# Two-layer decoder trunk on one Trainium2 core: four small matmul groups of the first mixer in another order on TensorE

## The chip, the cores and the metric

The kernel runs on one core of a Trainium2 chip, as one launch. The core has five engines that each work through a queue of their own: TensorE (PE, matmuls), VectorE (DVE), ScalarE (ACT), GpSimd (POOL) and SyncE (SP), which here only issues transfers (DMA). They wait for each other through semaphores. The metric is the device time of one execution in microseconds (us); less is better.

## The reference

The input is one sequence of 1024 tokens with 1024 features. Layer 0 has a mixer of two kinds of heads, eight retention heads and eight RWKV-7 heads of 64 features; layer 1 has sliding-window attention. Each layer ends in a SwiGLU network, and all of it is in float32. The change touches only the RWKV-7 heads of layer 0:

```python
def rwkv7_scan(r, w, k, v, a, b):
    def step(state, inp):
        r_t, w_t, k_t, v_t, a_t, b_t = inp
        sa = jnp.einsum('bhij,bhj->bhi', state, a_t)
        state = state * w_t[:, :, None, :] + sa[..., None] * b_t[:, :, None, :] + v_t[..., None] * k_t[:, :, None, :]
        return state, jnp.einsum('bhij,bhj->bhi', state, r_t)
    ...
# in the mixer, behind the shared input projection z = h @ w_in:
y = rwkv7_scan(r_h, heads(decay), k_h, v_h, -kk, kk * heads(a))
y = head_group_norm(y, RWKV_GN_EPS, ln_g, ln_b)
...
return jnp.concatenate([ret_out, rwkv_out], axis=-1) @ w_out
```

The state update of one token needs that of the token before. The kernel doesn't step through tokens: it takes chunks of 64 tokens, turns the updates inside a chunk into small products and one triangular solve, and carries the state from chunk to chunk.

## The kernel before

The 1024 tokens are worked on in two halves of 512 (`hf` 0 and 1). The eight RWKV heads of a half are four pairs `p`; two heads of 64 features fill the 128 partitions (rows), one head in rows 0 to 63, the other in rows 64 to 127 (`half`). Two pairs of one half make a unit `u`: units 0 and 1 are half 0, units 2 and 3 are half 1. A half has `NCH` = 8 chunks.

`pair` (one call for each of the eight pairs) makes, in this order on TensorE: the two small projections of decay and gate (tiles 0 and 1), a sum over each head's features (2), the chunk products of BK and AR called N here (3), which a masking on DVE and transfers through memory (`dn`) bring to the solve, the product of r with `blk` (4), the score groups, two for each half of the chunks, one for each head `e` (tiles 5, 6 and 7, 8; DVE masks them into GG at L887), the transposes of BK for either head (9, 10; ACT copies them into GG at L894), AR's transposition by a product with the identity (11; ACT copies it into `XA[:, :, 0:64]` at L901), the transposes of v (12, 13; DVE makes UV of them at L910 to L930), and GG by UV (14; ACT copies it into the other half of XA at L941).

`unit` solves the triangular systems of its two pairs by 62 steps on DVE, L968 and L972 in turn, on a tile X. Each step needs the one before it. The solved X goes to memory by two stores (`dg<-X`, L976) and comes back in another shape by eight loads (`GT<-dg`, L985); the unit's products with XA, UV and GG follow, and the state goes from chunk to chunk. Retention (lines about L1100 to L1240) runs in streams of its own: L1178 and L1193 are DVE's work between its matmuls, L1215 updates its state Sc, and L1240 stores a result (`cat<-r`). L581 makes normalized input `n` of the second half on DVE for the shared input projection, whose matmuls (`ps_f<-n,w`) fill TensorE between all this. Its split weights are kept in memory (`wsp`) and come back for the second half by L412 (`w<-wsp`).

What sets the order of the work:

- On TensorE, one list written out by hand, `PE_ORDER`. A letter is a stream: F the projection, a the first norm, b to e the units 0 to 3, f and g the pairs of unit 0, h and i those of unit 1, j and k of unit 2, l and m of unit 3, n to q and r to u retention in the first and the second half, v the second norm, W the output projection. `f3:16` takes sixteen matmuls from the fourth tile of stream f; `f5,6:8` takes eight, from the tiles 5 and 6 in turn. `pe_order` chains them in that order.
- A class `Plan` runs the streams as Python generators. It sets in which order instructions and tiles come into being in the program; it keeps an estimate of the time (`now`) and of the PSUM banks in use (`banks`) for that.
- On DVE, ACT, POOL and SP the framework's scheduler sets the order, by a cost estimate of its own, with a few pins in `pe_order`. Small tiles of PSUM come in turn from four banks named `ps_m`.

The helper `mm` (L293) issues a matmul, and `tr` (L304) a transpose.

Of the kernel before, what the change touches and what calls it, by code (L numbers as in the profile page):

```python
# [103 lines left out]

PE_ORDER = """
F0:13 F1:2 F0:3 F1:14 F0:3 F1:3 F0:3 F1:3 F0:2 F1:2 F2:2 a0:1 F2:22 F3:24 f0:1 f1:1 F4:24 F5:24 F6:15 f2:1 F6:9
F7:24 g0:1 g1:1 F8:9 f3:16 F8:9 g2:1 F8:6 F9:18 f4:1 F9:6 F10:6 f5,6:8 f7,8:8 F10:17 f9:8 f10:8 f11:16 f12:4
g3:16 f13:4 n0:4 n1:4 g4:1 F10:1 F11:12 f14:16 g5:1 g6:2 g5:2 g6,5:3 g7:1 g8:2 g7:2 F11:12 F12:3 g8,7:3 g9:8
g10:8 F12:13 g11:16 g12:4 n2,3:8 g13:4 F12:8 F13:5 n4:8 n5:8 F13:16 n6:8 g14:16 F13:3 F14:21 n7:1 F14:3 F15:24
F16:6 o0:4 o1:4 F16:18 F17:3 o2,3:8 o4:8 F17:21 o5:1 o6:1 o5:7 b0:32 o6:7 h0:1 h1:1 F18:18 b1:32 o7:1 F18:6  # L110
F19:12 b2:8 h2:1 b3:8 b4:8 F19:12 b5:8 b6:16 b7:8 b8:8 F20:24 F21:13 b9:16 b10:8 h3:16 b11:8 b12:4 F21:8 i0:1
i1:1 b13:4 F21:3 F22:24 F23:6 b14:4 i2:1 F23:6 b20:1 b15:4 b20:15 b21:6 b16:4 b21:4 b22:16 b23:5 F23:9 b23:1
b21:2 b17:4 b23:6 h4:1 F23:3 F24:11 b21:1 b18:4 b21:1 b23:2 h5:4 b21:1 b19:4 b21:1 b23:2 F24:12 h6:4 b24:1 F24:1
F25:24 F26:7 b25:1 b26:1 h7:4 h8:4 b27:1 h9:8 F26:11 h10:8 h11:16 h12:4 i3:16 h13:4 p0:4 F26:6 F27:9 p1:4 i4:1
p2:2 p3:2 p2,3:4 h14:16 i5,6:4 i5:2 i6:2 i7:4 i8:4 F27:15 F28:2 p4:8 i9:8 i10:8 F28:6 i11:16 i12:4 p5:8 p6:8
i13:4 F28:16 F29:19 v0:1 p7:1 i14:16 F29:5 F30:7 q0:4 q1:4 F30:3 F31:2 F30:3 F31:11 q2,3:8 F30:9 F31:6 F30:2
F31:2 q4:8 q5:8 F31:3 F32:6 q6:8 F32:18 F33:22 q7:1 c0:32 F33:2 F34:23 c1:32 F34:1 F35:20 c2:8 c3:8 c4:8 j0:1
F35:4 F36:11 j1:1 c5:8 c6:16 c7:8 c8:8 j2:1 F36:9 c9:16 c10:8 c11:8 c12:2 F36:4 F37:10 c12:2 F37:14 F38:7 j3:5
c13:4 j3:11 k0:1 k1:1 F38:8 c20:5 c14:4 c20:11 c21:6 c22:1 c21:2 c15:4 c22:15 c23:4 c21:2 c23:1 c16:4 c23:5 k2:1
F38:9 F39:8 c17:4 c21:2 c23:2 j4:1 F39:16 F40:2 c21:1 c18:4 c21:1 c23:2 j5:4 c21:1 c19:4 c21:1 c23:2 F40:3 j6:4  # L120
F40:19 F41:12 c24:1 F41:12 F42:24 c25:1 c26:1 j7,8:8 c27:1 j9:8 F43:13 j10:8 j11:16 j12:4 k3:16 j13:4 k4:1
F43:11 F44:11 j14:16 k5,6:8 k7:4 k8:4 F44:9 k9:8 k10:8 k11:16 k12:4 r0:4 r1:4 F44:4 F45:10 k13:4 r2,3:8 r4:8
F45:12 k14:16 r5:8 r6:8 l0:1 l1:1 F45:2 F46:17 r7:1 l2:1 F46:7 F47:24 m0:1 m1:1 F48:24 F49:1 l3:1 F49:17 d0:1
l3:3 d0:31 l3:12 m2:1 d1:32 F49:6 F50:15 d2:8 d3,4:16 d5:8 F50:9 F51:2 d6:16 d7:8 m3:16 d8:8 d9:16 d10:8 d11:8
F51:8 s0,1:8 d12:4 F51:14 F52:2 d13:4 F52:19 s2:1 d14:4 s3,2:7 F52:3 F53:3 d15:4 s4:8 F53:18 s5:2 d16:4 s6:8
d20:3 s5:6 d17:4 d20:13 d21:13 d18:4 d21:1 d22:16 d23:3 d21:1 d19:4 d21:1 d23:13 l4:1 F53:3 F54:14 m4:1 s7:1
l5:3 l6:3 l5:1 l6:1 d24:1 F54:10 F55:17 d25:1 d26:1 F55:7 F56:9 l7:4 l8:4 d27:1 l9:8 l10:8 l11:16 l12:4 m5:3
m6:3 m5:1 m6:1 l13:4 F56:15 m7:2 m8:2 m7,8:4 m9:8 m10:8 t0:4 t1:4 F57:24 m11:16 m12:4 t2:4 e0:2 t3:4 l14:16
m13:4 t4:8 t5:8 t6:4 e0:4 m14:1 t6:4 m14:15 e0:26 F58:24 F59:15 t7:1 e1:32 u0:4 u1:4 F59:9 W0:7 e2:8 e3:8 e4:8
u2:4 W0:17 W1:11 u3:4 e5:8 u4:8 e6:16 e7:8 e8:8 u5:8 u6:8 e9:16 e10:8 e11:8 e12:2 u7:1 e20:5 e12:2 e20:11 e21:4  # L130
e22:6 e13:4 e22:10 e23:4 e21:2 e14:4 e23:2 W1:13 W2:14 e15:4 e21:1 W2:10 W3:13 e21:1 e23:2 e21:1 e16:4 e21:1
e23:2 W3:11 W4:9 e17:4 e21:2 e23:2 W4:15 W5:4 e21:1 e18:4 e21:1 e23:2 W5:20 e19:4 e21:2 W6:24 W7:3 e23:2 e24:1
e25:1 e26:1 e27:1 W7:21
"""


# [121 lines left out]
class Kern:  # L258
# [520 lines left out]
    def pair(self, u, hf, p):  # L779


        nc, mp = self.nc, self.mp
# [118 lines left out]
        S.copy(XA[:, :, 0:64], ps)  # L901
# [1148 lines left out]
```

## Time and profile before

| what | number |
| --- | --- |
| time, median of 3 runs | 2292.93 us |
| lowest and highest | 2291.54 and 2293.13 us |
| the profiled execution | 2291.26 us |
| its span in the profile | 2289.4 us |
| mean granted clock of TensorE | 0.999 |
| first mixer, about | 0 to 640 us |

The profile is of one execution, and all its times count from the span's start. A row of a timeline has the start, the length, the engine, the line, the operation, output and inputs, the tile on TensorE (rows*columns) and the shape, the number of records, and in brackets the idle time before it and what ended it. A view of waits has the engine and tile that waited, what it waited for, the total in us, how many times, and the longest. Windows list what each engine was busy for in a stretch. SPq is the queue of transfers that SP issues.

### The profile page before, as it was taken

Reading aid. Unit: us, or ns where it says so; the run is one execution under the profiler, and the core shown is the slowest. Engines: PE = TensorE matmul, PEld = TensorE weight load, DVE = VectorE, ACT = ScalarE, POOL = GpSimd, SP = SyncE. Lnnn points to the kernel's source line nnn. Section 1 sums busy time; section 2 is a strip of 40 time slices with the busy share of each in tenths; the row PEclk is TensorE's granted clock in tenths of the full one; section 3 lists DMA queues with packets and bytes.
Section 4 is the critical chain, followed back from the end, with each engine's and each line's share of the span. In section 5 each row is a group of like instructions: output and inputs, shape, how many; then the busy total and the mean of one; then the engine's idle time right before and its main releaser. Section 6 shows DMA issues by size and latency. Waiting matters only on the chain.

```text
span 2289.4 us, 35743 instructions
## 1 busy us (share of the span) xinstructions
PE 2259.3 (99%) x13056; PEld 1808.5 (79%) x13056; DVE 1699.6 (74%) x2635; ACT 1047.6 (46%) x1947; POOL 1009.2 (44%) x796
## 2 busy tenths in 40 slices
PE   8999999999999999999999999999999999999998
PEld 6777777778878888888788887787788888888886
DVE  7877965876567268887895958857657788888866
ACT  5454544434445333334343466657744333333335
POOL 3123221212340167777776501113203677777675
PEclk9999999999999999999999999999999999999999
DMA  7566554444356455565756332133246466657663
GB/s 279 187 214 210 193 163 128 145 119 132 134 185 221 170 177 205 203 212 211 280 212 239 110 120 79 44 99 118 93 140 230 169 217 213 210 196 284 230 216 116
DMA packets 170336, 406.43 MB, mean 178 GB/s; under 512 B 43184, under 2 KB 45872, under 8 KB 170160
## 3 DMA queue, kind: packets, MB, share of 16 engines
q1 hardware_dynamic: 166752, 397.59, 50.7%
q10 hardware_dynamic: 2832, 4.45, 0.5%
q8 instruction: 104, 1.70, 0.3%
q0 software_dynamic: 576, 2.10, 0.2%
q14 instruction: 72, 0.59, 0.1%
HBM read 275.48 MB, written 123.21 MB: 174 GB/s over the span
## 4 chain that ended last, share of the span: by engine, by line
PE 79%; DVE 10%; ACT 4%; issue 3%; DMA 2%; SPq 1%; POOL 1%; DVEq 0%; ACTq 0%; POOLq 0%
PE ps_f L293 10%; PE ps_m L1302 7%; PE ps_m L1304 7%; PE ps_m L1305 7%; PE ps_m L293 6%; PE ps_f L1302 5%; PE ps_f L1304 5%; PE ps_f L1305 5%; PE ps_f L452 2%; PE ps_f L449 2%; PE ps_f L451 2%; PE ps_r L1302 2%; PE ps_c L1305 2%; PE ps_r L1304 2%; PE ps_c L1304 2%
## 5 line engine op out<-in xcount | busy, mean ns | idle before, releaser
L293 PE MATMUL ps_f<-n,w 128*128 128x512 f32 x1440 | 359.2, 403 | 8.3 <-ACT w L434 5.7
L293 PEld LDWEIGHTS ps_f<-n,w 128*128 128x128 f32 x1440 | 267.4, 189 | 83.0 <-issue 12.6
L435 POOL TENSOR_TENSOR w<-wr,w 128x512 fp32r<-128x512 f32 x63 | 87.0, 1388 | 301.4 <-ACT w L434 293.7
L434 ACT CAST w<-wr 128x512 fp32r<-128x512 f32 x231 | 141.2, 617 | 162.2 <-PE ps_f L452 54.2
L435 DVE TENSOR_TENSOR w<-wr,w 128x512 fp32r<-128x512 f32 x168 | 118.8, 710 | 61.4 <-ACT w L434 60.8
L1302 PE MATMUL ps_f<-n,w 128*128 128x512 f32 x415 | 164.3, 396 | 0.0
L1304 PE MATMUL ps_f<-n,w 128*128 128x512 f32 x415 | 162.7, 392 | 0.0
L1305 PE MATMUL ps_f<-n,w 128*128 128x512 f32 x415 | 162.5, 392 | 0.0
L435 POOL TENSOR_TENSOR w<-wq,w 128x512 fp32r<-128x512 f32 x91 | 130.8, 1448 | 30.9 <-ACT w L434 30.9
L1302 PE MATMUL ps_m<-n,w 128*128 128x512 f32 x333 | 130.4, 392 | 0.0
L1304 PE MATMUL ps_m<-n,w 128*128 128x512 f32 x333 | 129.7, 389 | 0.0
L1305 PE MATMUL ps_m<-n,w 128*128 128x512 f32 x333 | 129.5, 389 | 0.0
L1312 DVE TENSOR_TENSOR nq<-ps_m,u 128x512 f32<-128x512 f32 x88 | 58.9, 684 | 93.8 <-PE ps_m L1305 93.8
L1732 POOL TENSOR_SCALAR s<-s,st 128x256 f32<-128x256 f32 (+1 forms) x32 | 30.7, 961 | 191.1 <-ACT w L434 60.9
L466 POOL TENSOR_TENSOR n<-nq,n 128x512 fp32r<-128x512 f32 x60 | 100.0, 1679 | 7.6 <-ACT n L464 7.6
L1497 POOL TENSOR_TENSOR w<-wd,w 128x512 fp32r<-128x512 f32 (+1 forms) x62 | 87.7, 1423 | 33.5 <-ACT w L1496 31.5
L1302 PEld LDWEIGHTS ps_f<-n,w 128*128 128x128 f32 x415 | 77.9, 188 | 20.4 <-issue 3.8
L1302 PE MATMUL ps_m<-cb,w 128*128 128x512 f32 x236 | 91.9, 389 | 0.4 <-DVE nq L1312 0.4
L1304 PEld LDWEIGHTS ps_f<-n,w 128*128 128x128 f32 x415 | 77.9, 188 | 17.7 <-issue 2.0
L1305 PE MATMUL ps_m<-cb,w 128*128 128x512 f32 x236 | 91.8, 389 | 0.0
L1304 PE MATMUL ps_m<-cb,w 128*128 128x512 f32 x236 | 91.8, 389 | 0.0
L1305 PEld LDWEIGHTS ps_f<-n,w 128*128 128x128 f32 x415 | 77.9, 188 | 16.8 <-issue 0.7
(521 smaller groups left out, 6498.6 us busy)
## 6 DMA issues: line engine op xcount, KB each, us to landing
hc<-n SPq DMA_DIRECT2D x84, 512.0 KB, 3.2
wsp<-w SPq DMA_DIRECT2D x54, 512.0 KB, 3.3
w<-wsp SPq DMA_DIRECT2D x54, 512.0 KB, 3.4
n<-hc SPq DMA_DIRECT2D x54, 512.0 KB, 6.2
wq<-in_w_gate SPq DMA_DIRECT2D x44, 512.0 KB, 4.6
u<-u SPq DMA_DIRECT2D x88, 256.0 KB, 3.3
ha<-hc SPq DMA_DIRECT2D x34, 512.0 KB, 5.3
hid<-n SPq DMA_DIRECT2D x66, 256.0 KB, 2.1
```

The lines of the kernel that those rows point to most:

```text
L293: i = self.nc.tensor.matmul(out, lhsT, rhs, **kw)
L434: nc.scalar.copy(hi[:, :n], raw[:, c])
L435: self.lo.tensor_tensor(out=lo[:, :n], in0=raw[:, c], in1=hi.bitcast(F32)[:, :n], op=ALU.subtract)
L449: x = nc.tensor.matmul(ps, hi, rh, start=k == 0, stop=False)
L451: y = nc.tensor.matmul(ps, hi, rl, start=False, stop=False)
L452: z = nc.tensor.matmul(ps, lo, rh, start=False, stop=k == n - 1)
L466: e.tensor_tensor(out=lo, in0=src, in1=hi.bitcast(F32), op=ALU.subtract)
L1302: i = mm(ps, hi, xh, start=first and k == 0, stop=False, skip_group_check=True)
L1304: mm(ps, hi, xl, start=False, stop=False, skip_group_check=True)
L1305: mm(ps, lo, xh, start=False, stop=last and k == len(w) - 1, skip_group_check=True)
L1312: self.last_add = V.tensor_tensor(out=o, in0=x, in1=y, op=ALU.add)
L1497: nc.gpsimd.tensor_tensor(out=lo, in0=v, in1=hi.bitcast(F32), op=ALU.subtract)
```

## The change

The change rewrites the order of some small groups on TensorE, for the eight pairs.

- In pair h tiles 7 and 8, in i tiles 5 and 6, in k tiles 7 and 8, in l and m both groups: score matmuls of the two heads are issued in turn, where they stood apart. In pair g a group that was nearly in turn now is so.
- In f, g, i, k, l and m the transposes of BK (tiles 9 and 10) are issued in turn. In h and j they stay apart.
- In all eight pairs AR's transposition leaves its place behind BK's transposes. It moves behind the transposes of v and is issued in turn with GG by UV. One of its matmuls takes rows and columns of the first head or of the second, one of GG by UV takes rows of one head and columns of the other: four different quarters of TensorE come one after another. The tiles are numbered anew for it: 11 and 12 are v's transposes, 13 AR, 14 GG by UV. Both copies into XA now follow on ACT.
- The lines with `banks` and `now` keep `Plan`'s estimate as it was, so that the rest of the program comes into being in the same order. The instructions are the same, and so are their shapes.

```diff
-F7:24 g0:1 g1:1 F8:9 f3:16 F8:9 g2:1 F8:6 F9:18 f4:1 F9:6 F10:6 f5,6:8 f7,8:8 F10:17 f9:8 f10:8 f11:16 f12:4
-g3:16 f13:4 n0:4 n1:4 g4:1 F10:1 F11:12 f14:16 g5:1 g6:2 g5:2 g6,5:3 g7:1 g8:2 g7:2 F11:12 F12:3 g8,7:3 g9:8
...
+F7:24 g0:1 g1:1 F8:9 f3:16 F8:9 g2:1 F8:6 F9:18 f4:1 F9:6 F10:6 f5,6:8 f7,8:8 F10:17 f9,10:16 f11:4 g3:16 f12:4
+n0:4 n1:4 g4:1 F10:1 F11:12 f13,14:32 g5,6:8 g7,8:5 F11:12 F12:3 g7:1 g8:2 g9,10:16 F12:13 g11:4 n2,3:8 g12:4
...
-        XA = self.t(mp, [P, NCH, P], "XA", 2)
-        ps = self.pst("m", [P, NCH, 64])
-        for c in range(NCH):
-            for rs in half:
-                self.mm(ps[rs, c, :], AR[rs, c, 0:64], ident[rs, rs], start=True, stop=True)
-        S.copy(XA[:, :, 0:64], ps)
+        self.plan.banks.append(self.plan.now + 3.0)
+        for _ in range(2 * NCH):
+            self.plan.now += max(0.05, 0.00167 * 64 * 0.6)
...
-        ps = self.pst("m", [P, NCH, 64])
+        XA = self.t(mp, [P, NCH, P], "XA", 2)
+        pa, ps = (self.pst("m", [P, NCH, 64]) for _ in range(2))
+        self.plan.banks.pop()
+        now = self.plan.now
+        for c in range(NCH):
+            for e in range(2):
+                b = half[1 - e]
+                self.mm(pa[half[e], c, :], AR[half[e], c, 0:64], ident[half[e], half[e]], start=True, stop=True)
+        self.plan.now = now
         for c in range(NCH):
             for e in range(2):
                 b = half[1 - e]
                 self.mm(ps[half[e], c, :], GG[b, c, e, 0:64], UV[b, c, e, :], start=True, stop=True)
+        S.copy(XA[:, :, 0:64], pa)
         self.at["xa", hf, p] = S.copy(XA[:, :, 64:P], ps)
```

Three places show what this does to the engines' orders. The first is TensorE in pair f (its AR is AR_525, its BK is BK_529; AR_700 and BK_704 are pair g's, rv holds v). Before:

```order
L304 MATMUL ps_m_787<-c_ident_154,BK_529 128x64 x8
L304 MATMUL ps_m_797<-c_ident_154,BK_529 128x64 x8
L293 MATMUL ps_m_811<-c_ident_154,AR_525 64x64 x16
L304 MATMUL ps_m_830<-c_ident_154,rv_424 128x128 x4
L293 MATMUL ps_m_842<-AR_700,BK_704 64x64 x16
...
L293 MATMUL ps_m_980<-UV_829,GG_756 64x64 x16
```

and after, where the first two rows come eight times in turn, and the last two sixteen times:

```order
L303 MATMUL ps_m_787<-c_ident_154,BK_529 128x64
L303 MATMUL ps_m_797<-c_ident_154,BK_529 128x64
...
L303 MATMUL ps_m_811<-c_ident_154,rv_424 128x128 x4
L292 MATMUL ps_m_823<-AR_700,BK_704 64x64 x16
...
L292 MATMUL ps_m_962<-c_ident_154,AR_525 64x64
L292 MATMUL ps_m_963<-UV_810,GG_756 64x64
```

Sixteen matmuls on AR have left the place ahead of g's N, and stand among those of GG by UV.

The second place is the end of unit 1's solve, on DVE and on SP. DVE before (X_2530 is the solve's tile; its last step is the one with 128x16; lines from here on are by 1 or by 5 higher after):

```order
L972 TENSOR_TENSOR X_2530<-X_2530,xt_2534 128x12x8
L435 TENSOR_TENSOR w_3100<-wr_3015,w_3100 128x512
L435 TENSOR_TENSOR w_3103<-wr_3015,w_3103 128x512
L1193 TENSOR_TENSOR r_486_3044<-ps_m_3034,c_dmask_2980 128x512
L968 TENSOR_TENSOR xt_2534<-X_2530,DT_2527 128x91
L1193 TENSOR_TENSOR r_487_3046<-ps_m_3035,c_dmask_2980 128x512
L972 TENSOR_TENSOR X_2530<-X_2530,xt_2534 128x13x7
```

and after:

```order
L1183 SCALAR_TENSOR_TENSOR r_479_2999<-rvm_2997,ps_m_2992 128x512
L434 TENSOR_TENSOR w_3100<-wr_3015,w_3100 128x512
L977 TENSOR_TENSOR X_2511<-X_2511,xt_2515 128x16
L434 TENSOR_TENSOR w_3103<-wr_3015,w_3103 128x512
L1198 TENSOR_TENSOR r_486_3044<-ps_m_3034,c_dmask_2980 128x512
L1198 TENSOR_TENSOR r_487_3046<-ps_m_3035,c_dmask_2980 128x512
```

The last step of the solve stands ahead of both retention products (L1193 before, L1198 after); before, fourteen steps stood behind the first of them. SP at the same place, before:

```order
L1240 DMA cat_82<-r_434_2753 128x512
L708 DMA nq_6458<-cat_82 128x512
L364 DMA c_qdec_4241<-in_cst 128x128
L404 DMA wr_6520<-in_w_out 128x1024
L364 DMA c_dmask_4239<-in_cst 128x256
L412 DMA w_3169<-wsp 128x1024
L412 DMA w_3171<-wsp 128x1024
L976 DMA dg_215<-X_2530 1024x1x32 x2
L412 DMA w_3250<-wsp 128x1024
L985 DMA GT_3088<-dg_215 32x8x32 x4
```

and after:

```order
L1245 DMA cat_82<-r_432_2734 128x512
L981 DMA dg_215<-X_2511 1024x1x32 x2
L707 DMA nq_6458<-cat_82 128x512
L403 DMA wr_6520<-in_w_out 128x1024
L363 DMA c_dmask_4220<-in_cst 128x256
L363 DMA c_qdec_4222<-in_cst 128x128
L990 DMA GT_3088<-dg_215 32x8x32 x4
L990 DMA GT_3089<-dg_215 32x8x32 x4
L411 DMA w_3169<-wsp 128x1024
L411 DMA w_3171<-wsp 128x1024
```

The solve's two stores and eight loads have moved ahead of the weight loads w_3169 and w_3171.

The third place is SP at the end of unit 2's solve (dg_217). Before:

```order
L976 DMA dg_217<-X_4087 1024x1x32 x2
L1240 DMA cat_83<-r_673_4410 128x512
L412 DMA w_4705<-wsp 128x1024
L985 DMA GT_4582<-dg_217 32x8x32 x4
L985 DMA GT_4583<-dg_217 32x8x32 x4
L412 DMA w_4707<-wsp 128x1024
```

and after:

```order
L981 DMA dg_217<-X_4068 1024x1x32
L1245 DMA cat_83<-r_673_4410 128x512
L981 DMA dg_217<-X_4068 1024x1x32
L411 DMA w_4705<-wsp 128x1024
L990 DMA GT_4582<-dg_217 32x8x32 x4
L990 DMA GT_4583<-dg_217 32x8x32 x4
```

Retention's store `cat` has moved between the two stores of X. From the second norm on, all five engines' orders are those of before.

More of the change, by code (lines that the diff above doesn't have):

```diff
@@ L106 @@
 F0:13 F1:2 F0:3 F1:14 F0:3 F1:3 F0:3 F1:3 F0:2 F1:2 F2:2 a0:1 F2:22 F3:24 f0:1 f1:1 F4:24 F5:24 F6:15 f2:1 F6:9
-F7:24 g0:1 g1:1 F8:9 f3:16 F8:9 g2:1 F8:6 F9:18 f4:1 F9:6 F10:6 f5,6:8 f7,8:8 F10:17 f9:8 f10:8 f11:16 f12:4
-g3:16 f13:4 n0:4 n1:4 g4:1 F10:1 F11:12 f14:16 g5:1 g6:2 g5:2 g6,5:3 g7:1 g8:2 g7:2 F11:12 F12:3 g8,7:3 g9:8
-g10:8 F12:13 g11:16 g12:4 n2,3:8 g13:4 F12:8 F13:5 n4:8 n5:8 F13:16 n6:8 g14:16 F13:3 F14:21 n7:1 F14:3 F15:24
-F16:6 o0:4 o1:4 F16:18 F17:3 o2,3:8 o4:8 F17:21 o5:1 o6:1 o5:7 b0:32 o6:7 h0:1 h1:1 F18:18 b1:32 o7:1 F18:6
@@ L111 @@
[L111 to L130, printed above, removed]
@@ L131 @@
-e22:6 e13:4 e22:10 e23:4 e21:2 e14:4 e23:2 W1:13 W2:14 e15:4 e21:1 W2:10 W3:13 e21:1 e23:2 e21:1 e16:4 e21:1
-e23:2 W3:11 W4:9 e17:4 e21:2 e23:2 W4:15 W5:4 e21:1 e18:4 e21:1 e23:2 W5:20 e19:4 e21:2 W6:24 W7:3 e23:2 e24:1
-e25:1 e26:1 e27:1 W7:21
+F7:24 g0:1 g1:1 F8:9 f3:16 F8:9 g2:1 F8:6 F9:18 f4:1 F9:6 F10:6 f5,6:8 f7,8:8 F10:17 f9,10:16 f11:4 g3:16 f12:4
+n0:4 n1:4 g4:1 F10:1 F11:12 f13,14:32 g5,6:8 g7,8:5 F11:12 F12:3 g7:1 g8:2 g9,10:16 F12:13 g11:4 n2,3:8 g12:4
+F12:8 F13:5 n4:8 n5:8 F13:16 n6:8 g13,14:32 F13:3 F14:21 n7:1 F14:3 F15:24 F16:6 o0:4 o1:4 F16:18 F17:3 o2,3:8
@@ new lines @@
+o4:8 F17:21 o5:1 o6:1 o5:7 b0:32 o6:7 h0:1 h1:1 F18:18 b1:32 o7:1 F18:6 F19:12 b2:8 h2:1 b3:8 b4:8 F19:12 b5:8
+b6:16 b7:8 b8:8 F20:24 F21:13 b9:16 b10:8 h3:16 b11:8 b12:4 F21:8 i0:1 i1:1 b13:4 F21:3 F22:24 F23:6 b14:4 i2:1
+F23:6 b20:1 b15:4 b20:15 b21:6 b16:4 b21:4 b22:16 b23:5 F23:9 b23:1 b21:2 b17:4 b23:6 h4:1 F23:3 F24:11 b21:1
+b18:4 b21:1 b23:2 h5:4 b21:1 b19:4 b21:1 b23:2 F24:12 h6:4 b24:1 F24:1 F25:24 F26:7 b25:1 b26:1 h7,8:8 b27:1
+h9:8 F26:11 h10:8 h11:4 i3:16 h12:4 p0:4 F26:6 F27:9 p1:4 i4:1 p2:2 p3:2 p2,3:4 h13,14:32 i5,6:8 i7,8:8 F27:15
@@ new lines @@
+F28:2 p4:8 i9,10:16 F28:6 i11:4 p5:8 p6:8 i12:4 F28:16 F29:19 v0:1 p7:1 i13,14:32 F29:5 F30:7 q0:4 q1:4 F30:3
+F31:2 F30:3 F31:11 q2,3:8 F30:9 F31:6 F30:2 F31:2 q4:8 q5:8 F31:3 F32:6 q6:8 F32:18 F33:22 q7:1 c0:32 F33:2
+F34:23 c1:32 F34:1 F35:20 c2:8 c3:8 c4:8 j0:1 F35:4 F36:11 j1:1 c5:8 c6:16 c7:8 c8:8 j2:1 F36:9 c9:16 c10:8
+c11:8 c12:2 F36:4 F37:10 c12:2 F37:14 F38:7 j3:5 c13:4 j3:11 k0:1 k1:1 F38:8 c20:5 c14:4 c20:11 c21:6 c22:1
+c21:2 c15:4 c22:15 c23:4 c21:2 c23:1 c16:4 c23:5 k2:1 F38:9 F39:8 c17:4 c21:2 c23:2 j4:1 F39:16 F40:2 c21:1
@@ new lines @@
+c18:4 c21:1 c23:2 j5:4 c21:1 c19:4 c21:1 c23:2 F40:3 j6:4 F40:19 F41:12 c24:1 F41:12 F42:24 c25:1 c26:1 j7,8:8
+c27:1 j9:8 F43:13 j10:8 j11:4 k3:16 j12:4 k4:1 F43:11 F44:11 j13,14:32 k5,6:8 k7,8:8 F44:9 k9,10:16 k11:4 r0:4
+r1:4 F44:4 F45:10 k12:4 r2,3:8 r4:8 F45:12 k13,14:32 r5:8 r6:8 l0:1 l1:1 F45:2 F46:17 r7:1 l2:1 F46:7 F47:24
+m0:1 m1:1 F48:24 F49:1 l3:1 F49:17 d0:1 l3:3 d0:31 l3:12 m2:1 d1:32 F49:6 F50:15 d2:8 d3,4:16 d5:8 F50:9 F51:2
+d6:16 d7:8 m3:16 d8:8 d9:16 d10:8 d11:8 F51:8 s0,1:8 d12:4 F51:14 F52:2 d13:4 F52:19 s2:1 d14:4 s3,2:7 F52:3
@@ new lines @@
+F53:3 d15:4 s4:8 F53:18 s5:2 d16:4 s6:8 d20:3 s5:6 d17:4 d20:13 d21:13 d18:4 d21:1 d22:16 d23:3 d21:1 d19:4
+d21:1 d23:13 l4:1 F53:3 F54:14 m4:1 s7:1 l5,6:8 d24:1 F54:10 F55:17 d25:1 d26:1 F55:7 F56:9 l7,8:8 d27:1
+l9,10:16 l11:4 m5,6:8 l12:4 F56:15 m7,8:8 m9,10:16 t0:4 t1:4 F57:24 m11:4 t2:4 e0:2 t3:4 l13,14:32 m12:4 t4:8
+t5:8 t6:4 e0:4 t6:4 m13,14:32 e0:26 F58:24 F59:15 t7:1 e1:32 u0:4 u1:4 F59:9 W0:7 e2:8 e3:8 e4:8 u2:4 W0:17
+W1:11 u3:4 e5:8 u4:8 e6:16 e7:8 e8:8 u5:8 u6:8 e9:16 e10:8 e11:8 e12:2 u7:1 e20:5 e12:2 e20:11 e21:4 e22:6 e13:4
@@ L134 @@
+e22:10 e23:4 e21:2 e14:4 e23:2 W1:13 W2:14 e15:4 e21:1 W2:10 W3:13 e21:1 e23:2 e21:1 e16:4 e21:1 e23:2 W3:11
+W4:9 e17:4 e21:2 e23:2 W4:15 W5:4 e21:1 e18:4 e21:1 e23:2 W5:20 e19:4 e21:2 W6:24 W7:3 e23:2 e24:1 e25:1 e26:1
+e27:1 W7:21
 """
```

## The prediction

> **What bounds the kernel now.** I read the page's busy times and its chain first. They say that TensorE is the engine that sets the end, and that little of its time is free.
>
> ```profile
> PE 2259.3 (99%) x13056; PEld 1808.5 (79%) x13056; DVE 1699.6 (74%) x2635; ACT 1047.6 (46%) x1947; POOL 1009.2 (44%) x796
> PE 79%; DVE 10%; ACT 4%; issue 3%; DMA 2%; SPq 1%; POOL 1%; DVEq 0%; ACTq 0%; POOLq 0%
> ```
>
> By these two lines alone, a microsecond taken off TensorE is a microsecond off the run. But 10% of the chain runs through DVE, so I then cut the first mixer into stretches with the view of windows. The columns are the length, then the busy time (and records) of PE, its weight loads, DVE, ACT and POOL, then clock, DMA share and GB/s.
>
> ```profile
> 93.00:144.00 51.00, 49.34 (x383) 39.12 (x384) 46.10 (x115) 18.94 (x31) 10.77 (x12) 1.00 0.65 210
> 238.00:294.00 56.00, 52.70 (x433) 40.54 (x433) 53.84 (x125) 27.37 (x42) 16.51 (x14) 1.00 0.62 198
> 294.00:384.00 90.00, 90.00 (x828) 69.74 (x827) 45.99 (x89) 41.46 (x60) 17.51 (x30) 1.00 0.46 142
> 403.00:443.00 40.00, 39.09 (x293) 30.18 (x291) 38.18 (x101) 14.34 (x23) 11.03 (x16) 1.00 0.40 121
> 503.00:553.00 50.00, 49.95 (x459) 38.95 (x458) 30.25 (x62) 17.93 (x27) 6.70 (x5) 1.00 0.46 136
> ```
>
> In three of these, in which the solves of units 0, 1 and 2 run, DVE is busy for 46.10 of 51 us, 53.84 of 56 and 38.18 of 40, and PE is the engine with holes. At 294 to 384 and 503 to 553 it is the other way round. The view of waits, and the timeline of PE, say who holds PE up in those three:
>
> ```profile
> PE ps_m L293 <- DVE r L1193: 2.0, 4, 1.3
> PE ps_f L293 <- DVE n L581: 1.7, 2, 1.0
> 283.00 1.20 PE L293 MATMUL ps_f<-n,w 128*128 128x512 f32 x4 [0.73 <-DVE n L581]
> 286.08 0.43 PE L293 MATMUL ps_m<-r,r 128*64 128x128 f32 x2 [1.26 <-DVE r L1193]
> 291.16 6.21 PE L293 MATMUL ps_f<-n,w 128*128 128x512 f32 x26
> 447.22 1.65 PE L293 MATMUL ps_f<-n,w 128*128 128x512 f32 x6 [0.18 <-DMA w<-wsp]
> ```
>
> A saving on PE just ahead of such a wait only lengthens the wait, unless DVE comes earlier too. So I price the change twice: what it takes off PE, and what of it passes these places.
>
> **What it takes off PE.** These are PE's rows for the groups that change. A matmul in f32 leaves two records here, a transpose one; a group's length is the distance to the next group's start, since the ends overlap.
>
> ```profile
> 79.82 1.01 PE L304 MATMUL ps_m<-c_ident,BK 64*128 64x64 f32 x16
> 80.77 1.15 PE L293 MATMUL ps_m<-c_ident,AR 64*64 64x64 f32 x32
> 81.84 0.66 PE L304 MATMUL ps_m<-c_ident,rv 128*128 128x128 f32 x4
> 88.94 1.15 PE L293 MATMUL ps_m<-UV,GG 64*64 64x64 f32 x32
> 225.35 1.71 PE L293 MATMUL ps_m<-AR,BK 64*128 64x128 f32 x16
> 226.99 1.12 PE L293 MATMUL ps_m<-gl,gup 128*128 128x512 f32 x2
> 384.65 1.16 PE L293 MATMUL ps_m<-AR,BK 64*128 64x128 f32 x16
> 385.74 1.13 PE L293 MATMUL ps_m<-gl,gup 128*128 128x512 f32 x2
> ```
>
> *Score groups.* Eight score matmuls with the row halves apart (225.35, pair h) last until 226.99: 1.64 us. With the halves in turn (384.65, pair j) they last 1.09. Where a pair's group goes from apart to in turn, 0.55 is saved; h has one such group, i, l and m two, k one. Parts of these blocks overlap already by their order, so I take 0.55 for h, 0.55 for i, 0.5 for k, 0.85 for l and 0.35 for m: 2.8 us.
>
> *BK's transposes.* No trace shows them in turn. Apart, sixteen last 0.95 (79.82 to 80.77). If in turn they gain what the scores gain, a third goes (1.09 of 1.64): 0.32 for each pair. The ends are 0 (transposes of different halves might not run together) and 0.48 (perfect overlap, half of 0.95). I take 0.32, nearest to the score rows, for the six pairs: 1.9 us.
>
> *AR's transposition.* Today its sixteen matmuls cost 1.07 us of their own (80.77 to 81.84), and GG by UV about the same. After the change 32 matmuls run in four quarters. Whether four quarters run side by side is the question, and one place of the trace shows it by accident, where retention's r by Sc (two quarters) meets GG by UV (the two others):
>
> ```profile
> 113.95 0.28 PE L293 MATMUL ps_m<-r,Sc 64*64 64x128 f32 x2
> 113.96 0.28 PE L293 MATMUL ps_m<-UV,GG 64*64 64x64 f32 x4
> 114.06 0.28 PE L293 MATMUL ps_m<-r,Sc 64*64 64x128 f32 x2
> 114.07 0.28 PE L293 MATMUL ps_m<-UV,GG 64*64 64x64 f32 x4
> ```
>
> Six records start every 0.11 us: four of UV,GG at 28 ns each, no slower than the 34 they take alone (1.08 over 32 records), with two of r,Sc beside them. So the joint group should last about 1.1 us, and the other 1.07 is saved in each of eight pairs, less some 0.05 for a slower start: 8.2 us. The ends: 0 (see the rival on quarters) and 8.6.
>
> The Trainium skill, TensorEngine Tiling (Array Packing), section Gotcha 1: PSUM Pressure, speaks against it: different row tiles cannot access the same PSUM bank at one time, and here both row halves write into AR's tile, and both into GG·UV's. By that rule at most two quarters would be at work, the group would last 2.15 us, and the sum on PE would lose the 8.2. The trace speaks against the rule in this use: the UV,GG row at 88.94 has both row halves writing one tile and reaches 34 ns a record.
>
> Together 2.8 + 1.9 + 8.2 = 12.9 us come off PE, 0.56% of the run. The change adds no instruction; AR's copy on ACT moves from the pair's transposes to its GG·UV, where XA's other copy is, and ACT has room (27.37 of 56 us in the densest stretch). Its duration:
>
> ```profile
> L901 ACT COPY XA<-ps_m 128x512 f32<-128x512 f32 x8 | 4.7, 588 | 6.1 <-PE ps_m L293 6.1
> ```
>
> XA is read only in the unit's products later, so its later birth is hidden by the solve; where the solve did not come last, it would cost one such copy, 0.59 us a unit. The banks ("m", four) are taken in a slightly other turn; where both transposes' banks open together, the second comes free later, at most by one ACT copy; I cost this at nothing where DVE has room, and let it eat a part of l and m below.
>
> **What passes the saturated stretches.** The diff moves nothing on DVE, POOL, ACT and SP by itself, but their orders come from a scheduler that sees the earlier PE, and they have changed.
>
> *Up to 225 us.* f's and g's savings (2 × 1.02 + 2 × 0.32) are 2.7. Unit 0's solve has DVE full from 93 on, but its steps stand nearly as before; with part of g's gain held at L1178 and L917 I keep 1.9.
>
> *Unit 1's solve (238 to 294).* Pair i's N scores, which the solve waits for, come 1.9 + 0.55 (h's scores) + 1.02 (AR of h, no longer ahead of them) = 3.5 us earlier, so the solve starts that much earlier. But in the new order all the solve's steps stand ahead of the two L1193, of which the old order had fourteen behind the first. Their rows and the transfers that hang on them:
>
> ```profile
> 285.34 0.68 DVE L1193 TENSOR_TENSOR r<-ps_m,c_dmask 128x512 f32<-128x512 f32 x1
> 285.94 0.24 DVE L968 TENSOR_TENSOR xt<-X,DT 128x91 f32<-128x91 f32 x1
> 292.26 0.18 DVE L972 TENSOR_TENSOR X<-X,xt 128x16 f32<-128x16 f32 x1
> 287.23 1.95 SPq L412 DMA_DIRECT2D w<-wsp  x2
> 292.47 1.53 SPq L976 DMA_DIRECT2D dg<-X  x2
> 295.98 3.78 SPq L985 DMA_DIRECT2D GT<-dg  x8
> ```
>
> Fourteen steps of 0.24 down to 0.18 us, 0.21 in the mean, are 2.9 us, and 3.1 with some gaps between dependent steps. So L1193 comes 3.5 − 3.1 = 0.4 us earlier than today, and since PE waits there (286.08) PE's lead is cut to 0.4, whatever h and i saved. Ends: 3.5 (if the steps fill holes of DVE that the old order had) and −2 (if the lead of the solve is 1.5 us smaller).
>
> On SP the same shift puts the two stores dg<-X and the eight GT<-dg ahead of the load w<-wsp that stood ahead of them. X's last step would end near 285.34 + 3.1 − 3.5 − 0.6 = 284.3, dg issues then; from dg's issue to GT's the old rows have 295.98 − 292.47 = 3.5, less the 0.5 of SP's other issues that now fall inside it, and the eight GT take 3.78: the load is issued at about 291.1 in place of 287.23. These loads took a median of
>
> ```profile
> w<-wsp SPq DMA_DIRECT2D x54, 512.0 KB, 3.4
> ```
>
> 3.4 us over the run, so it lands at 294.5 or, if the small packets of GT slow it by 1.5 us, 296.0. PE needs it after the eighteen matmuls that the projection before still has at 291.16, so at 291.16 + 18 × 6.21/26 = 295.5, or 295.1 with the lead of 0.4. I take a wait of 0.5, the middle of the two (ends 0 and 0.9 of them; 3.5 if the lead isn't there). At 296 us the balance is −0.4 + 0.5 = +0.1.
>
> *Unit 2's solve (403 to 443).* Savings of j and k (1.02 × 2, 0.5, 0.32) are 2.9, most of them ahead of PE's waits for DVE, where the new order has the awaited rows a few places earlier: about 1.4 stays at 425. But SP's order goes from dg, dg, cat to dg, cat, dg:
>
> ```profile
> 436.00 1.29 SPq L976 DMA_DIRECT2D dg<-X  x2
> 437.39 0.63 SPq L1240 DMA_DIRECT2D cat<-r  x1
> 439.39 3.77 SPq L985 DMA_DIRECT2D GT<-dg  x8
> 443.27 4.12 SPq L412 DMA_DIRECT2D w<-wsp  x4
> ```
>
> The second dg (436.65 today) now stands behind cat, which issued at 437.39, so it issues near 438.0: 1.3 later. GT waits for it, the load w<-wsp is behind GT, and PE waits for that load at 447.22 with no slack. So the 1.4 is gone and 1.3 is added: +1.3 for this stretch (ends: −1.4, if cat comes earlier as PE does; +2.0, if X's last steps, which stand behind three more foreign rows of about 0.2 each, come later too).
>
> *l and m (503 to 553).* DVE has 20 us of room and PE none. AR 2 × 1.02, scores 0.85 + 0.35, transposes 2 × 0.32 are 3.9; the second pair of score banks and the copies of the banks hold back about a third of it, as they hold the sixteen transposes at 526.47 to 1.40 us today against 0.95 elsewhere:
>
> ```profile
> 526.47 1.47 PE L304 MATMUL ps_m<-c_ident,BK 64*128 64x64 f32 x16
> 527.87 1.15 PE L293 MATMUL ps_m<-c_ident,AR 64*64 64x64 f32 x32
> ```
>
> I keep 2.7 (ends 0 and 3.9). Behind the first mixer the orders are as before.
>
> The sum: +0.1 + 1.3 − 2.7 = −1.3 us. The profiled execution took 2291.26 us, 1.9 more than its span of 2289.4, so 2290.0 for one like it; the median of the runs stands 1.67 above that execution, so 2291.6 against 2292.93: 0.06% less, within the 0.2% (4.6 us) below which I call it no change, about what a measurement of this kernel tells from none.
>
> **The rivals.**
>
> *The savings flow through.* For it: PE is 99% busy, and L1193, L581, L1178 and the like, the waits that eat them, are under 10 us in all. Where DVE's holes take the fourteen steps, h, i, j and k keep theirs as well. All of it gives 2292.93 − 12.9 = 2280.0; half of it, if one of the two later solves holds, about 2286.5. Against it: 53.84 us of 56 leaves DVE 2.2 us of holes, less than the 3.1 to be put in. Chance 0.30.
>
> *The quarters do not overlap* (the rule above, or PE keeping its order so that a waiting quarter holds the others): the joint group lasts 2.15 us and 8.2 fall out of the sum. Then N of pair i comes 1.5 earlier, not 3.5, and L1193 1.6 later than today; with l and m at 0.9, +1.6 + 0.5 + 1.3 − 0.9 = +2.5: 2295.4, still no change. Against it: the rows at 113.95. Chance 0.08.
>
> *Slower: the lead never forms.* The scheduler's new order costs its price wherever the solve does not start earlier. If the four banks or the transfers of DT, not PE, set the start of the solves, X ends at 287.8, w<-wsp issues near 294.6 and lands at 298 to 299 where PE needs it at 295.5: +3.5 at unit 1; unit 2 is at its end of +2.0; and the banks that held the lead hold l and m too, gain 0. That is +5.5, 2298.4. It decides from a lead of the solve of less than about 1 us in place of 3.5. For it: PE's rows in these stretches have waits on DVE, which the banks go through. Chance 0.17.
>
> **How the numbers follow.** My own sum has the rest, 0.45, and its time is the prediction, 2291.6; its own range, by the ends of its terms, is 2288.5 to 2295.5. To hold 8 in 10 the range reaches half way into the first rival and to the last one's price: 2286.0 to 2298.0. Faster by over 0.2%: 0.30. Within: 0.45 + 0.08 = 0.53. Slower: 0.17.
>
> **What would show it.** In the trace after: the joint group of c_ident,AR and UV,GG about 1.1 us long (2.15 would be the second rival); score groups with 16 records at 1.09; sixteen transposes at 0.63; the waits for L1193 and L581 (2.0 and 1.7 us today) grown by some two us together, and PE less than a us ahead at 296; a wait for w<-wsp near 295 and a larger one near 448; l and m together some 3 us shorter. I am wrong if PE does the work of today's 296 us some 3 us earlier, or if the four quarters slow each other.

## The result and the profile after

The changed kernel takes 2297.27 us (median of 20 runs, 2294.85 to 2302.81) against 2291.86 us (20 runs, 2289.74 to 2295.17) of the kernel before: 1.0023 times, 95% interval 1.0016 to 1.0029, so about 5.3 us slower. The forecast was 1.3 us faster. The time lies inside the stated range, on the side to which I had given 0.17.

The profiled execution took 2295.16 us. Its page, span and busy times:

```profile
span 2293.4 us, 35737 instructions
...
PE 2252.1 (98%) x13056; PEld 1800.2 (78%) x13056; DVE 1700.1 (74%) x2635; ACT 1045.9 (46%) x1947; POOL 1009.3 (44%) x796
```

TensorE is busy 7.2 us less than before (2259.3 to 2252.1), of the 12.9 that the prediction took off it; some 3.4 of the rest were lost to stretches at half clock (last section). But it stands idle for 41.3 us of the span in place of 30.1, 11.2 more, and 11.2 − 7.2 is the 4.0 us by which the span grew. The view of what TensorE waited for in the first mixer, and its timeline at the largest of these waits:

```profile
...
PE ps_m L303 <- DVE GG L886: 4.7, 6, 2.3
PE ps_f L292 <- DMA w<-wsp: 2.9, 2, 1.9
PE ps_m L292 <- DVE Sc L1220: 2.7, 2, 2.3
PE ps_m L292 <- ACT XA L945: 2.4, 1, 2.4
PE ps_f L292 <- DVE n L580: 2.1, 2, 1.4
PE ps_m L292 <- DVE r L1198: 1.8, 4, 1.2
```

```profile
232.04 3.69 PE L292 MATMUL ps_f<-n,w 128*128 128x512 f32 x15
...
243.61 2.08 PE L292 MATMUL ps_m<-AR,BK 64*128 64x128 f32 x16 [2.38 <-ACT XA L945]
...
286.39 0.43 PE L292 MATMUL ps_m<-r,r 128*64 128x128 f32 x2 [1.18 <-DVE r L1198]
...
293.26 0.44 PE L292 MATMUL ps_m<-r,Sc 64*64 64x128 f32 x4 [2.33 <-DVE Sc L1220]
...
410.87 0.27 PE L303 MATMUL ps_m<-c_ident,BK 64*128 64x64 f32 x1 [2.30 <-DVE GG L886]
...
448.91 0.47 PE L292 MATMUL ps_f<-n,w 128*128 128x512 f32 x1 [0.97 <-DMA w<-wsp]
454.23 1.66 PE L292 MATMUL ps_f<-n,w 128*128 128x512 f32 x6 [1.88 <-DMA w<-wsp]
```

Before, none of the masks into GG, the updates of Sc, ACT's copies into XA and the loads w<-wsp held TensorE up for more than 0.2 us. I laid the matmuls of the input projection, which are the same in both kernels, side by side by their number. How much later the changed kernel issues the same matmul, by the time of before:

| time before | 85 | 196 | 235.7 | 246.5 | 287.9 | 291.2 | 375.6 | 395.0 | 409.8 | 423.7 | 447.8 | 511.7 | 553.7 | 2235 |
| --- | --- | --- | --- | --- | --- | --- | --- | --- | --- | --- | --- | --- | --- | --- |
| later by, us | −1.9 | −2.3 | −3.6 | +1.0 | +0.2 | +3.2 | +3.2 | +2.2 | +5.2 | +4.1 | +7.0 | +6.7 | +4.7 | +4.8 |

The lead of 3.6 us forms as forecast. It is lost at 243, 3 us more go at 293, and 3 us each at 410 and at 444 to 454. Three views of other queues in the changed kernel show what was waited for. ACT at 243:

```profile
242.45 0.63 ACT L674 ACTIVATE nq<-nq 128x512 f32<-128x512 f32 x1 [2.24 <-DMA nq<-in_xT]
242.99 0.57 ACT L945 COPY XA<-ps_m 128x512 f32<-128x512 f32 x1
243.45 0.59 ACT L946 COPY XA<-ps_m 128x512 f32<-128x512 f32 x1
```

The two copies that free the banks for pair i's scores stand behind a square that waits for a load. DVE at 293:

```profile
287.46 0.26 DVE L1220 SCALAR_TENSOR_TENSOR Sc<-Sc,c_gam,ps_m 128x64 f32<-128x64 f32 x1
292.61 0.43 DVE L1000 STREAM_TRANSPOSE TZ<-GT 32x256 f32<-32x256 f32 x1 [4.89 <-DMA GT<-dg]
292.98 0.23 DVE L1220 SCALAR_TENSOR_TENSOR Sc<-Sc,c_gam,ps_m 128x64 f32<-128x64 f32 x1
```

The second update of Sc stands behind a transpose of GT, which the transfers have not yet brought, and DVE stands still for 4.89 us. SP in unit 2, first where DT is loaded, then where X is stored:

```profile
398.55 1.80 SPq L853 DMA_DIRECT2D dn<-DT  x4
400.45 0.40 SPq L411 DMA_DIRECT2D w<-wsp  x1
401.61 1.13 SPq L962 DMA_DIRECT2D DT<-dn  x2
...
441.96 0.58 SPq L981 DMA_DIRECT2D dg<-X  x1
442.60 0.65 SPq L1245 DMA_DIRECT2D cat<-r  x1
443.29 0.57 SPq L981 DMA_DIRECT2D dg<-X  x1
```

A weight load of 512 KB starts ahead of DT, and the store `cat` stands between the two stores of X, which was in the prediction. The solve's first step follows DT. In the changed kernel, on DVE, and then in the kernel before, on SP and DVE:

```profile
407.79 0.19 DVE L973 TENSOR_TENSOR xt<-X,DT 128x31 f32<-128x31 f32 x1 [4.40 <-DMA DT<-dn]
```

```profile
398.41 1.13 SPq L957 DMA_DIRECT2D DT<-dn  x2
403.14 0.19 DVE L968 TENSOR_TENSOR xt<-X,DT 128x31 f32<-128x31 f32 x1 [2.27 <-DMA DT<-dn]
```

From DT's issue to that step it takes 6.2 us (401.61 to 407.79); it took 4.7 before. The masks L886, for which TensorE waits at 410.87, stand behind the solve's first ten steps on DVE; before, the masks L887 stood behind the first nine, so TensorE waits mainly because the solve starts 4.65 us later, while TensorE itself is only 2.2 us later here.

### The profile page after: what moved, and what is told of

Its sections match the earlier page's. It is cut to its first block, busy times and chain, and to the rows that moved or that the text cites. A ratio compares the mean times of both kernels' runs of the same rounds, so it can differ in the third digit from the quotient of the medians.

```text
span 2293.4 us, 35737 instructions
## 1 busy us (share of the span) xinstructions
PE 2252.1 (98%) x13056; PEld 1800.2 (78%) x13056; DVE 1700.1 (74%) x2635; ACT 1045.9 (46%) x1947; POOL 1009.3 (44%) x796
## 4 chain that ended last, share of the span: by engine, by line
PE 77%; DVE 10%; ACT 4%; DMA 4%; issue 3%; SPq 1%; POOL 1%; DVEq 0%; ACTq 0%; POOLq 0%
PE ps_f L292 8%; PE ps_m L1307 7%; PE ps_m L1310 7%; PE ps_m L1309 7%; PE ps_f L1307 5%; PE ps_f L1309 5%; PE ps_f L1310 5%; PE ps_m L292 5%; PE ps_f L451 2%; PE ps_f L450 2%; PE ps_f L448 2%; PE ps_r L1307 2%; PE ps_c L1310 2%; PE ps_r L1310 2%; PE ps_r L1309 2%
```

## The experiments

To hold the queues, a kernel gets a table with the order of the first mixer's instructions for each of DVE, ACT, POOL and SP (as numbers of issue), and chains them as the TensorE list is chained. The tables make such a kernel's line numbers 60 to 77 higher than those of the kernel it comes from. With the changed kernel's own orders in them, the engines' orders are the changed kernel's: in the traces of e2, e3 and e4 the instructions of DVE, ACT, POOL and SP differ from its order by the edit alone.

```diff
     def pe_order(self):
...
+        for e, t in QUEUES.items():
+            ks = []
+            for w in t.split():
+                a, _, b = w.partition("-")
+                ks += range(int(a), int(b or a) + 1)
+            for i, j in zip(ks[1:], ks):
+                self.tc.add_manual_dep(qs[e][i], qs[e][j].name, ...)
```

The kernel before was run along with each group of four; the ratios are to those runs (their medians: 2291.67, 2291.80, 2292.34 and 2292.81 us).

| run | time, us | ratio to before | 95% interval |
| --- | --- | --- | --- |
| the changed kernel | 2297.27 | 1.0023 | 1.0016 to 1.0029 |
| e1 new TensorE order, old queues | 2287.92 | 0.9980 | 0.9971 to 0.9989 |
| e2 ACT square behind | 2296.47 | 1.0027 | 1.0016 to 1.0038 |
| e3 DVE transposes behind | 2294.48 | 1.0017 | 1.0008 to 1.0026 |
| e4 two transfers on SP | 2294.67 | 1.0013 | 1.0004 to 1.0022 |
| e5 as e1, BK's transposes apart | 2286.85 | 0.9976 | 0.9967 to 0.9986 |
| e6 quarters alone, old queues | 2288.67 | 0.9987 | 0.9978 to 0.9995 |
| e7 scores and transposes, old queues | 2290.76 | 0.9997 | 0.9988 to 1.0006 |
| e8 quarters alone, queues free | 2294.93 | 1.0011 | 1.0002 to 1.0020 |
| e9 e3 and e4 together | 2292.95 | 1.0006 | 0.9997 to 1.0015 |
| e10 as e1, but ACT's new order | 2288.83 | 0.9985 | 0.9977 to 0.9994 |
| e11 before, short solve | 2286.88 | 0.9975 | 0.9966 to 0.9984 |
| e12 e5 with short solve | 2282.66 | 0.9960 | 0.9948 to 0.9972 |
| e13 old TensorE order, new queues | 2299.82 | 1.0035 | 1.0022 to 1.0047 |
| e14 e9 and unit 1's loads | 2291.35 | 0.9993 | 0.9984 to 1.0001 |
| e15 e14 and the ACT square | 2290.91 | 0.9995 | 0.9986 to 1.0003 |
| e16 scores alone, old queues | 2291.15 | 0.9998 | 0.9989 to 1.0007 |

**TensorE's order or the queues' (e1, e13).** e1 keeps the changed TensorE list and gives the queues their old orders; e13 does the opposite.

```diff
-    "DVE": the changed kernel's order   (ACT, POOL, SP too)
+    "DVE": the order of the kernel before
```

> TensorE's order is the changed one, and DVE, ACT, POOL and SP issue the first mixer in the order of the kernel before (AR's copy into XA stands ahead of XA's other copy). Theory A, the queues: what costs time is that the scheduler's new orders put instructions that wait for a transfer ahead of some for which TensorE waits. Then the new waits of the changed kernel (2.4 us at 243.6, 2.7 at 293, 2.8 at 411, 2.9 at 449 to 454) go, and the saving on TensorE shows: 4 to 10 us faster than before, near 2285 us. Theory B, the PE order: two groups in turn need two banks at once, and TensorE stalls whatever the queues do: 2 to 6 us slower than before, as the changed kernel is.

> TensorE in the order of the kernel before, DVE, ACT, POOL and SP in the order of the changed kernel (AR's copy into XA stays at its old place on ACT). Theory A: the new queue orders cost what they cost with either order of TensorE, 9 us: near 2301 us. Rival: they are bad only together with the earlier TensorE; 2292 to 2296 us.

e1 is 0.20% faster than before (4.6 us by the ratio, 3.8 by the medians), at the lower end of what theory A gave, and so faster than both kernels. e13 is 0.35% slower than before, nearer to theory A's 2301 us than to the rival. So the new orders of the four queues cost 8 us with the old TensorE list (1.0035) and 9.9 us with the new one (1.0023 against 0.9980), and the new TensorE list gives 2.7 to 4.6 us. The loss is the queues' and not the list's. In e13 TensorE waits for the same things, though its own order is the old one (view of waits; only the waits for the masks are shorter there, 1.6 us in all in place of 4.7):

```profile
PE ps_m L356 <- ACT XA L1017: 2.4, 1, 2.4
PE ps_m L356 <- DVE Sc L1291: 2.1, 2, 1.8
PE ps_f L356 <- DMA w<-wsp: 2.0, 1, 2.0
```

**Which moves (e2, e3, e4, e9).** Each holds all queues in the changed kernel's orders and moves a few instructions.

```diff
 e2, ACT
-L674 nq_408<-nq_408
 L945 XA_409<-ps_m_410
 L946 XA_409<-ps_m_411
 L674 nq_401<-nq_401
+L674 nq_408<-nq_408
 e3, DVE (three of the four TZ; the fourth stands behind already)
 L1220 Sc<-Sc
-L1000 TZ<-GT
 L1220 Sc<-Sc
-L1000 TZ<-GT
...
 L1220 Sret<-Sc
+L1000 TZ<-GT  x3
 e4, SP
-L411 w_4428<-wsp
 L962 DT_4065<-dn_216  x2
+L411 w_4428<-wsp
...
-L1245 cat_83<-r_673
 L981 dg_217<-X_4068
+L1245 cat_83<-r_673
```

> The changed kernel with all queues held, but for one ACT instruction: the square nq<-nq (L674, the input's load lands at 242.45) stands behind the two copies into XA of pair h instead of ahead of them. A: the wait of 2.4 us at 243.6 is gone; since DVE is full from 238 to 288, only 0 to 1 us of it reaches the end. A rival A2 says that the solve itself hangs on this place: the whole 2.4 us reach the end. B: the wait stays, because the banks are full for other reasons; no difference.

> The changed kernel with all queues held, but for three DVE instructions: the transposes TZ<-GT of unit 1 (L1000, they wait for GT<-dg) stand behind the four updates of Sc (L1220) instead of among them. A: the waits of 2.3 and 0.3 us for Sc at 293 to 294 go and are not given back: 2.2 to 2.7 us faster than the changed kernel. B: no difference over 0.5 us.

> The changed kernel with all queues held, but for two SP instructions of unit 2: one load w<-wsp stands behind DT<-dn instead of ahead of it, and the store cat<-r behind the second dg<-X instead of ahead of it. A: DT lands 1.4 us earlier, the second dg issues 0.7 to 1.3 us earlier, and the run is 1.5 to 2.7 us faster than the changed kernel. B: no difference over 0.5 us.

> The changed kernel with all queues held, but for both mends: the three TZ transposes of unit 1 behind the updates of Sc on DVE, and the two transfers of unit 2 put back on SP. Theory A: the two gains add (2.8 and 2.6 us alone): 2291 to 2293 us, level with the kernel before. Rival: one takes the place of the other, 2294 us or more.

e2 makes no difference that these runs resolve (2296.47 against 2297.27), though its wait is gone: TensorE then waits for a mask at 249.75 (1.69 us) and for Sc at 255.42 (1.54 us), and DVE, busy for 48.71 of the 50 us from 238 to 288, sets the pace there, as expected. By the medians e3 takes 2.8 us off and e4 2.6, near what theory A gave; by the ratios it is 1.4 and 2.3, and both intervals overlap that of the changed kernel, so neither gain is sure by itself. Together, in e9, they are clear of the changed kernel: 4.3 us off by the medians, 3.9 by the ratios, level with before. Five instructions on two queues undo the loss. That Sc's wait would not be given back was expected and is not so. In e3 and e9 TensorE no longer waits for Sc, and meets a wait that the changed kernel's profile does not have at this place. TensorE in e3, then TensorE and SP in e9:

```profile
297.98 5.29 PE L354 MATMUL ps_f<-n,w 128*128 128x512 f32 x22 [1.46 <-DMA w<-wsp]
```

```profile
296.91 3.38 PE L354 MATMUL ps_f<-n,w 128*128 128x512 f32 x9 [1.77 <-DMA w<-wsp]
```

```profile
284.61 1.30 SPq L1056 DMA_DIRECT2D dg<-X  x2
...
288.17 5.04 SPq L1065 DMA_DIRECT2D GT<-dg  x8
293.31 8.56 SPq L486 DMA_DIRECT2D w<-wsp  x5
```

This is the prediction's wait for unit 1's weights behind GT; in the changed kernel it was hidden by the longer wait for Sc.

**Unit 1's loads, and the square again (e14, e15).**

```diff
 e14 = e9 and, on SP
+L411 w_3169<-wsp
+L411 w_3171<-wsp
 L990 GT_3088<-dg_215  x4
 L990 GT_3089<-dg_215  x4
-L411 w_3169<-wsp
-L411 w_3171<-wsp
 e15 = e14 and the move of e2
```

> As the run with both mends, and on SP the two loads w<-wsp of unit 1 stand ahead of the eight GT<-dg instead of behind them. The term of the prediction: the wait for w<-wsp near 296 (1.8 us in that run's profile) goes, and little of it comes back as a later GT: 1 to 2 us faster, 2291 to 2292 us. Rival: the wait passes to GT and the unit's products behind it, no difference over 0.5 us.

> As that run, and on ACT the square nq<-nq behind both copies into XA of pair h. With the other waits gone, A: the wait of 2.3 us at 243 goes and 0 to 1.5 us of it reach the end: 2290 to 2291.5 us, better than the kernel before.

e14 is 1.6 us faster than e9 by the medians (3 by the ratios, whose intervals overlap), and clear of the changed kernel. In its profile the wait at 296 is gone, and TensorE passes the place without a hole:

```profile
289.93 1.09 PE L354 MATMUL ps_m<-r,Sc 64*64 64x128 f32 x16
290.95 9.38 PE L354 MATMUL ps_f<-n,w 128*128 128x512 f32 x40
```

e15 is not told apart from e14. What is left between e14 and e1 (0.13%, their intervals overlap) lies in moves that no run took singly, among them the solve's steps on DVE that stand ahead of L1198; e10, with the old orders on DVE, POOL and SP and the new one on ACT, was expected at 2288 to 2289 us if ACT has no part in it, and 2288.83 us, within the interval of e1, says so.

**The parts (e5, e6, e7, e8, e16).** All but e8 have the queues in the old orders. The TensorE lists differ from that of e1 so:

```diff
 e5:  BK's transposes apart
-f9,10:16
+f9:8 f10:8        (g, i, k, l, m too)
 e6:  as e5, and the scores as before
-h7,8:8
+h7:4 h8:4         (g, i, k, l, m too)
 e7:  scores and transposes in turn, AR at its old place
 e8:  e6 without the tables
 e16: e7 with the transposes apart
```

> As the run with the old queues, but BK's transposes of the two heads stand apart again, as before the change. Theory C, the banks: transposes in turn need the second bank at their first step, and TensorE waits for the mask that frees it (4.1 us of waits for GG in all in that run, none before); apart, eight transposes cover it. Then this is 0.5 to 1.5 us faster than with the transposes in turn, near 2287 us. Rival: what they save (0.3 us for each of six pairs) outweighs the waits, and this is 0.5 to 1.5 us slower.

> AR's transposition in turn with GG by UV alone; scores and transposes of BK as before, and DVE, ACT, POOL and SP in the order of the kernel before. TensorE is spared about 8 us. Theory A: with the old queues it can't lose, and some 2 to 4 us pass the stretches in which DVE sets the pace: 2287.5 to 2289.5 us. Theory B (two banks opened together stall TensorE): no gain, 2291 us or more.

> The kernel before, its queues held in their order, with score groups and BK's transposes in turn and AR where it was. TensorE is spared 4.7 us at most. Theory A: 0.5 to 2 us faster than before. Theory C: the waits for the second bank eat all of it, 0.5 us faster to 1 us slower.

> The quarters alone as in the run of that name, but the queues left to the scheduler. Theory A, if AR's move is what turns the queues round: 2 to 6 us slower than before. If it takes the scores and transposes as well: at most 1 us slower.

> The kernel before with its queues held and the score groups alone in turn. TensorE is spared 2.1 us. With the transposes in turn as well the time was 1.0 us under that of before. Theory C (transposes in turn wait for their second bank and cost more than they save): this is 0.5 to 1.5 us faster than that, 2289.3 to 2290.3 us. Rival: the transposes' 1.9 us count, and this is 0.5 to 1 us slower than that, 2291 us or more.

The quarters are what gains: 3 us alone with held queues (e6, 0.9987). They are also enough to turn the queues round: left to the scheduler, the same change is 0.11% slower than before (e8). Scores alone and scores with transposes are not told apart from the kernel before. Whether the transposes in turn cost anything stays open: e5 stands 1.1 us under e1 and e7 0.4 us under e16, all within the intervals. e5 is the fastest kernel that computes everything, 2286.85 us, 5.5 us under before by its ratio.

**Does DVE take the rest (e11, e12)?** With the old queues about 5 us arrive (e5) of some 10 that this list spares TensorE, 8 by the quarters and 2 by the scores. To see whether DVE's full stretches take the others, both orders were run with 30 of the 62 steps of each solve left out; X is then not solved, and the two are compared with each other alone.

```diff
-        for j in range(31):
+        for j in range(16):
```

> The kernel before with its queues held, but each unit's solve does its first 32 of 62 steps (the later 30 are left out, so X is not solved). It spares DVE some 30 times 0.24 us in each of four units. It is the base for the run with the short solve and the new order; by itself: 2 to 6 us faster than before, since TensorE waits there for some 8 us in all.

> The new TensorE order without the transposes in turn, with the old queues, and with the short solve (30 of 62 steps of each unit left out, X not solved). Theory D, DVE's full stretches take the saving: with room on DVE, most of the 11 us spared on TensorE arrive, and this is 7 to 11 us faster than the short solve with the old order. Rival E, banks and latencies take it: 4 to 5.5 us faster, as with the full solve.

e12 is 4.2 us faster than e11 by the medians (3.4 by the ratios), about what E says and no more than with the full solve; theory D as it was priced falls. The load of the later 30 steps is not what takes the rest. DVE as such is not cleared: the first 32 steps stay, and DVE is still busy for 44.62 of the 50 us from 238 to 288 in e12 (48.99 in e5). The timelines show small waits that grow. In e11 and in e12, at the same matmul:

```profile
412.60 0.69 PE L354 MATMUL ps_m<-r,r 128*64 128x64 f32 x16 [0.53 <-DVE r L1255]
```

```profile
409.53 0.69 PE L352 MATMUL ps_m<-r,r 128*64 128x64 f32 x16 [1.18 <-DVE r L1259]
```

TensorE gets here 3.7 us earlier in e12 (408.35 in place of 412.07). But DVE works from the solve's first steps to this r with no wait in either run, and the whole row of that work, behind a transfer of DT, is only 3.07 us earlier (the solve starts at 397.31 in place of 400.39). So this wait, 0.65 us longer, is one for DVE where the solve starts. I read the rest as a sum of such waits; no run took them one by one, so this is argued, not shown.

## Why the prediction was wrong

Point by point, by its own steps:

- **Quarters: right.** The joint group lasts 1.09 us for 32 matmuls, and 1.09 to 1.12 in all pairs but h, where a wait of 0.48 us for DVE falls inside it. In the changed kernel, pair j, first record of the group and start of the next:

```profile
402.64 0.27 PE L292 MATMUL ps_m<-c_ident,AR 64*64 64x64 f32 x1
402.65 0.27 PE L292 MATMUL ps_m<-UV,GG 64*64 64x64 f32 x1
...
403.73 2.46 PE L292 MATMUL ps_m<-AR,BK 64*128 64x128 f32 x31
```

  So the rival on quarters fell, and with it the Trainium skill's rule in TensorEngine Tiling (Array Packing), Gotcha 1: PSUM Pressure, for this use: both row halves write both tiles, at 17 ns a record.
- **Scores: a little too large.** By the groups' lengths they save 2.1 us, not 2.8: i's two groups (7 and 8 are in turn now as well as 5 and 6) gave 0.34 (2.69 before, 2.35 in e1), k's nothing to speak of.
- **Transposes: right in size.** Sixteen in turn last 0.64 us (79.18 to 79.82, pair f, against 0.95 apart), the forecast was 0.63. They did not show at the end (e5, e7, e16).

```profile
79.18 0.71 PE L303 MATMUL ps_m<-c_ident,BK 64*128 64x64 f32 x16
79.82 0.66 PE L303 MATMUL ps_m<-c_ident,rv 128*128 128x128 f32 x4
```

- **The lead at unit 1's solve: right.** 3.6 us at 235.7 (232.04 in the row above), forecast 3.5; and at L1198 hardly any of it is left, 286.39 against 286.08, forecast 0.4 earlier. On the way it was lost in another manner than forecast: the waits for L1193 and L581, which I had said would grow by two us together, went from 2.0 and 1.7 to 1.8 and 2.1, and ACT's square held TensorE instead; e2 and e15 show no gain from moving it. The lower end that I gave for this lead, −2, is a wrong sum: 0.4 − 1.5 is −1.1.
- **Unit 1's weight loads: right place, too small.** I took 0.5 us. The wait came only when the one for Sc was gone, with 1.46 us (e3) and 1.77 us (e9), and taking it away gave 1.6 us by the medians (e14). The term was too small in the issue and not in the landing: in e9 the load is issued at 293.31 in place of 291.1, since X ends later (285.15 in the changed kernel, not 284.3) and the eight GT take 5.04 us of issues, not 3.78; TensorE goes on 3.6 us behind the issue, where I had 3.4. The slowing by 1.5 us that I allowed for stands in no row of this case.
- **Sc at 293: the step that failed.** "What passes the saturated stretches" priced the solve's steps, dg, GT and the loads; it did not price that TZ, which waits for GT, had been put among Sc's updates, for which TensorE waits. That cost 2.7 us of waits; 1.46 of them come back in e3 as the wait for the weights, which they had hidden, and at the end e3 gains 1.4 us by the ratios, 2.8 by the medians.
- **Unit 2: the second failure.** I had +1.3 for cat between the stores of X. TensorE loses 3.8 us from 375.6 to 447.8. The part not seen is the weight load ahead of DT, with which DT takes 1.5 us longer and the solve, and the masks behind its first steps, come later. e4 puts that load and cat back: DT to the solve's first step is 5.0 us there, and e4 gives back 2.6 by the medians, 2.3 by the ratios.
- **l and m: right.** 2.3 us come back between 480 and 554, forecast 2.7.

Term by term, from the table: +0.2 up to 288 (forecast −0.4), +3.0 to 375.6 (forecast +0.5, for the weights), +3.8 to 447.8 (forecast +1.3) and −2.3 to 553.7 (forecast −2.7) are +4.7 where the sum had −1.3. At the spans' ends 4.0 of it are left. The medians are 5.4 apart; the last section says what may be in the difference.

That the measured time lies inside the stated range is luck: the range reached up to the price of the slow rival, 2298.4, but that rival named a lead that never forms; the lead formed, and was lost to queue heads that wait for transfers. My own range, 2288.5 to 2295.5, is not what the ends of the terms give: added as stated they are −8.8 and +4.9, which is 2284.1 to 2297.8.

## What to carry to other kernels

When a scheduler sets the queues' order, a new order on one engine can be a new order on all, as it was here. Read the new orders for every instruction that waits for a transfer, and ask what now stands behind it for which the bounding engine waits; pricing by busy time does not find it (DVE was idle for 4.89 us of such a wait). Holding the other queues in their old order separates what a change gives from what the scheduler made of it, and here turned 0.23% slower into 0.20% faster (e1), and 0.24% with BK's transposes apart (e5).
